# RMSNorm with swish on one core: transfers of 4 MB in place of 2 MB, same ring, same compute pieces

## The chip, the cores and the metric

The kernel runs on one core of a Trainium2 chip. The metric is the device time of one execution in microseconds (us).

Engines: ACT (ScalarE), DVE (VectorE), POOL (GpSimd), SP (SyncE, which here only issues loads), and 16 DMA engines that move data between the chip's main memory and its on-chip memory. TensorE is not used.

## The reference

```python
# x: 16 x 1024 x 512 float32, gamma: 512 ones, eps = 1e-5
rms = np.sqrt(np.mean(x ** 2, axis=-1, keepdims=True) + eps)
x_norm = x / rms * gamma
return (x_norm * (1.0 / (1.0 + np.exp(-x_norm)))).astype(np.float32)
```

33.55 MB come in and 33.55 MB go out.

## The kernel before

The 16384 rows of 512 floats are cut into tiles. A tile of `sz` gives each of the 128 partitions `sz` neighbouring rows, so one partition's share is one contiguous run of `sz` x 2 KB, and a tile is `sz` x 256 KB. Tiles live in one ring of 96 rows per partition (24 MB). A tile is computed in place and stored from the same place. Compute goes in pieces of 4 rows per partition (1 MB), whatever the tile's size.

```python
    sizes = [4, 4] + [8] * 15      # 1, 1, then fifteen times 2 MB
    ring = 96
    ahead = 32
    cn = 4
    # ... (cut: tiles = (first row, size, place in the ring); chunks = places of the pieces)

    def load(t):                   # the SP queue
        nc.sync.dma_start(out=buf(t), in_=dram(xf, t))

    def store(t):                  # the ACT queue
        nc.scalar.dma_start(out=dram(of, t), in_=buf(t))

    # sums(k): 3 rows of squares on ACT, 1 on DVE.  root(k): DVE, then POOL (power -0.5)
    # norm(k): 4 DVE instructions.                  swish(k): one ACT instruction
    # ... (cut)
        for k in range(K + 3):
            if k < K:
                sums(k)
                root(k)
            while stored < len(tiles) and ends[stored] <= k - 2:
                store(stored)
                stored += 1
            # ... (cut: gamma at k == 0)
            if 1 <= k <= K:
                norm(k - 1)
            if 2 <= k < K + 2:
                swish(k - 2)
                # ... (cut: further loads, as far ahead as the ring allows)
```

ACT works in program order, so a store issue stands behind the sums of a later piece. And the framework shares eight completion semaphores (the counters by which an engine learns that a transfer has landed) among all transfers: a transfer whose semaphore was used before waits at its issue until that earlier transfer, on whichever queue, has landed. A listing of the built program's instructions with their waits shows which.

## Time and profile before

| what | before |
|---|---|
| time | 164.03 us (163.86 to 164.15) |
| span of the profiled run | 162.1 us |
| bytes moved, mean rate | 67.15 MB, 414 GB/s |
| ACT, DVE busy | 118.8 us, 110.3 us |
| transfers | 17 loads, 17 stores, and gamma |

From the page of the kernel before: the busy tenths of the engines and the rate of the DMA engines, each in 40 slices of 4.05 us.

```profile
DVE  0376999998996800970088978859998999998000
ACT  3447999999996009800799889499999999996300
```

In the DMA row, a 9 is 90% busy or more.

```profile
DMA  4999999999999999999999999999999999999992
GB/s 162 439 437 449 392 376 423 437 429 419 433 425 441 429 425 437 433 425 437 433 425 437 433 425 433 437 425 433 435 414 445 429 421 441 429 425 441 429 425 121
DMA packets 4908, 67.15 MB, mean 414 GB/s; under 512 B 548, under 2 KB 548, under 8 KB 552
```

The DMA engines are full in every slice but the first and the last. ACT and DVE have holes of several slices. So this is a kernel at the pace of its transfers. The dip to 376 GB/s in the fifth and sixth slices will come up again, with the kernel after_2m_start.

The view of waits of the kernel before (engine, line, what it waited for: total us, times, longest us):

```profile
POOL rstd L97 <- DVE aeps L93: 98.5, 32, 11.9
DVE aeps L93 <- ACT junk_a L80: 32.8, 32, 9.9
ACT xb L111 <- DMA xb<-in_x_dram: 21.2, 4, 9.6
ACT junk_a L80 <- DMA xb<-in_x_dram: 6.9, 4, 2.9
```

Two lines of its timeline (start us, duration us, engine and line; in brackets the idle time before it):

```profile
60.66 0.34 ACTq L73 DMA_DIRECT2D out_dram<-xb  x1
61.04 1.91 ACT L111 ACTIVATE xb<-xb 128x2048 f32<-128x2048 f32 x1 [8.12 <-DMA xb<-in_x_dram]
```

The third line of waits looks as if swish (L111) needed a load. It does not: its data had been on the chip long before. The timeline shows a store issue directly ahead of it on ACT, and the trace has the ninth load landing at 60.58 us. The listing of waits says the same: that store reuses the semaphore of that load. Below, such a load, on which a store waits only because of the shared semaphore, is called foreign. ACT stands still for 21 us in this way, and, as the DMA row says, it costs nothing.

### The profile page before, as it was taken

What the parts mean: (1) busy time and instruction counts of PE and PEld (TensorE: products, weight loads), DVE (VectorE), ACT (ScalarE), POOL (GpSimd) and SP (SyncE); (2) the same over time, 40 slices, a digit from 0 to 9 for tenths busy, and PEclk for the clock granted to TensorE, in tenths of its full rate; (3) what the DMA queues carried; (4) which work ended last, traced back from release to release, by engine and by line L of the source; (5) the groups of instructions that cost most, each with busy time, mean ns of one, the idle gap of its engine ahead of it and who ended that gap; (6) DMA issues with size and microseconds to landing.
All of it is one profiled execution on the core that took longest, in us unless ns stands there. A gap on an engine that the chain in (4) does not pass through costs nothing.

```text
span 162.1 us, 629 instructions
## 1 busy us (share of the span) xinstructions
DVE 110.3 (68%) x226; ACT 118.8 (73%) x225; POOL 46.4 (29%) x38
## 2 busy tenths in 40 slices
DVE  0376999998996800970088978859998999998000
ACT  3447999999996009800799889499999999996300
POOL 1052433333441300330033423333333444430000
DMA  4999999999999999999999999999999999999992
GB/s 162 439 437 449 392 376 423 437 429 419 433 425 441 429 425 437 433 425 437 433 425 437 433 425 433 437 425 433 435 414 445 429 421 441 429 425 441 429 425 121
DMA packets 4908, 67.15 MB, mean 414 GB/s; under 512 B 548, under 2 KB 548, under 8 KB 552
## 3 DMA queue, kind: packets, MB, share of 16 engines
q1 hardware_dynamic: 2448, 33.56, 49.3%
q10 hardware_dynamic: 2456, 33.56, 48.4%
q14 instruction: 4, 0.03, 0.0%
HBM read 33.56 MB, written 33.55 MB: 414 GB/s over the span
## 4 chain that ended last, share of the span: by engine, by line
DMA 47%; ACT 36%; issue 4%; DVE 3%; another core or an unknown queue 1%; SPq 0%; ACTq 0%; DVEq 0%
DMA xb<-in_x_dram 36%; ACT junk_a L80 19%; ACT xb L111 17%; DMA out_dram<-xb 12%; DVE xb L104 3%; SPq L70 0%; ACTq L73 0%; DVEq L178 0%; DVE aeps L93 0%; ACTq L80 0%
## 5 line engine op out<-in xcount | busy, mean ns | idle before, releaser
L104 DVE SCALAR_TENSOR_TENSOR xb<-xb,rstd,gamma_sb 128x512 f32<-128x512 f32 x128 | 87.4, 745 | 0.0
L111 ACT ACTIVATE xb<-xb 128x2048 f32<-128x2048 f32 x32 | 60.7, 1897 | 23.1 <-DMA xb<-in_x_dram 21.2
L97 POOL TENSOR_TENSOR rstd<-aeps,neg_half 128x4 f32<-128x4 f32 x32 | 45.6, 1426 | 98.5 <-DVE aeps L93 98.5
L80 ACT ACTIVATE junk_a<-xb 128x512 bf16<-128x512 f32 x96 | 58.9, 615 | 6.9 <-DMA xb<-in_x_dram 6.9
L93 DVE TENSOR_SCALAR aeps<-ms 128x4 f32<-128x4 f32 x32 | 5.4, 170 | 32.8 <-ACT junk_a L80 32.8
L86 DVE CUSTOM_DVE_ANT_0 junk_v<-xb 128x512 bf16<-128x512 f32 x32 | 21.9, 683 | 6.0 <-DMA xb<-in_x_dram 6.0
L80 ACT ACTIVATION_READ_ACCUMULATOR junk_a<-xb 128x1 f32 x96 | 18.0, 187 | 0.0
L117 ACT ACT_TABLE_LOAD x1 | 1.3, 1283 | 2.4 <-issue 2.4
L86 DVE DVE_READ_ACCUMULATOR2_ANT ms<- 128x1 f32 x32 | 2.6, 81 | 0.0
L140 DVE STREAM_SHUFFLE gamma_sb<-gamma 128x512 f32<-128x512 f32 x1 | 0.7, 724 | 0.0
L114 POOL MEMSET gamma<- 128x512 f32 x1 | 0.5, 525 | 0.3 <-POOLq L164 0.3
L164 POOL MEMSET const-float32-0.0<- 128x1 f32 x1 | 0.1, 99 | 0.2 <-issue 0.2
L115 POOL MEMSET neg_half<- 128x4 f32 x1 | 0.1, 103 | 0.0
L164 POOL MEMSET const-bfloat16-1.0<- 128x1 bf16 x1 | 0.1, 102 | 0.0
L164 POOL MEMSET const-uint8-127<- 128x1 uint8 x1 | 0.1, 102 | 0.0
L164 POOL MEMSET const-float32-1.0<- 128x1 f32 x1 | 0.1, 99 | 0.0
L140 DVE LOAD_MASK_SELECT gamma_sb<-gamma x1 | 0.0, 14 | 0.0
## 6 DMA issues: line engine op xcount, KB each, us to landing
xb<-in_x_dram SPq DMA_DIRECT2D x15, 2048.0 KB, 44.0
out_dram<-xb ACTq DMA_DIRECT2D x15, 2048.0 KB, 17.5
xb<-in_x_dram SPq DMA_DIRECT2D x2, 1024.0 KB, 5.8
out_dram<-xb ACTq DMA_DIRECT2D x2, 1024.0 KB, 14.5
gamma<-in_gamma_dram ACTq DMA_DIRECT2D x1, 8.0 KB
```

The lines of the kernel that those rows point to most:

```text
L80: nc.scalar.activation(out=junk[:], in_=row, func=AF.Square, accum_out=ms[:, k, j : j + 1],)
L86: nc.vector.tensor_tensor_reduce(out=junk[:], in0=row, in1=row, scale=1.0, scalar=0.0, op0=ALU.mult, op1=ALU.add, accum_out=ms[:, k, j : j ...
L93: nc.vector.tensor_scalar(out=aeps[:, k, :], in0=ms[:, k, :], scalar1=inv_d, scalar2=eps_f, op0=ALU.mult, op1=ALU.add,)
L97: nc.gpsimd.tensor_tensor(out=rstd[:, k, :], in0=aeps[:, k, :], in1=neg_half[:], op=ALU.pow)
L104: nc.vector.scalar_tensor_tensor(out=row, in0=row, scalar=rstd[:, k, j : j + 1], in1=gamma_sb[:], op0=ALU.mult, op1=ALU.mult,)
L111: nc.scalar.activation(out=rows, in_=rows, func=AF.Silu)
L114: nc.gpsimd.memset(gamma4[:], 0.0)
L115: nc.gpsimd.memset(neg_half[:], -0.5)
L117: nc.scalar.preload_act_table_set("silu_and_others")
L140: nc.vector.stream_shuffle(gamma_sb[:], gamma4[:], [0] * 32)
L164: nc = _bacc.Bacc("TRN2", target_bir_lowering=False, num_devices=1)
```

## The change

The intent: fewer and larger transfers for most of the data, small ones at the start so that compute begins early, 2 MB at the end so that the last store is short.

```diff
-    sizes = [4, 4] + [8] * 15
+    sizes = [4, 4, 8] + [16] * 6 + [8, 8]
     ring = 96
     ahead = 32
     cn = 4
```

Each partition's contiguous run goes from 16 KB to 32 KB in the six large tiles; the transfers go from 17 to 11 each way.

## The prediction

> **What bounds the kernel now.** The DMA engines, over nearly all of the 162.1 us span. The page's DMA row reads 9 in all but the end slices; 67.15 MB move at a mean of 414 GB/s. ACT is busy 73%, DVE 68%. The trace's packet records say it more finely: packets start at 1.74 us, all 16 engines stay occupied until about 159 us, loads end at 132.8 us, then stores alone run at about 430 GB/s. A 16 KB packet takes 611 ns, an 8 KB one 309 ns, on either queue: 16 x 16384 B / 611 ns = 429 GB/s. The Trainium skill ("DMA: Bandwidth & Descriptors", section "Where 436 GB/s comes from") puts a ceiling of 435 GB/s there; the trace agrees within 2%.
>
> **What the change does.** Same bytes, same compute pieces, same ring. Seventeen loads and seventeen stores become eleven and eleven; rows of 16 KB per partition become 32 KB for 24 of 32 MB each way.
> - Packet overhead: from 309 and 611 ns, about 7 ns of a packet is fixed (an estimate). If 32 KB goes as one packet it takes about 1215 ns: six tiles x 2 directions x 8 packets per engine x 7 ns = 0.7 us less. If it is cut at 16 KB, nothing.
> - Issue time (0.33 to 0.5 us each, timeline) falls, off the critical path.
> - 21.2 us of ACT's swish "waiting on loads" (longest 9.6 us, view of waits) are store issues held by a load far ahead that shares their semaphore (order listing). With fewer transfers these waits go; ACT waits for whole 4 MB loads instead. Both are off the critical path while a queue is full.
> - Sharing: the queues alternate by packet (8 KB stores against 16 KB loads ran at 133 and 270 GB/s; the skill's section "Queues, rings and completion order", same page, states it). So 4 MB loads outrun the small first stores, and 4 MB stores slow the last two loads.
>
> **Is any of it on the critical path?** Only if both queues empty. I laid out a timetable from these durations (per piece: ACT 1.84 us sums and 1.80 us swish, DVE 2.7 us, POOL 1.44 us; the packet times; the waits of the order listing). For the kernel before it gives the last landing at 161.3 us (measured 161.1). For after: the fourth tile lands at about 25 us (ACT waits 5 us); the last load at 134 us; the last 4 MB store cannot be issued before that, because sums that need that load stand ahead of it on ACT, so at about 134.5 us, while the store before it drains until about 139 us. The margin is about 5 us, so no hole; the last store is issued at 147 to 149 us with a 2 MB store still ahead of it, as before. Last landing: 160.6 us with 32 KB packets, 161.1 us with 16 KB.
>
> **Prediction.** 163.5 us, range 162.4 to 164.8. Faster by over 2%: 0.02; within 2%: 0.93; slower by over 2%: 0.05.
>
> **What would show it.** DMA row at 9 in all but the end slices; 32 KB packets near 1215 ns; loads ending at 132 to 134 us; the last 4 MB store issued just after the last load lands; ACT and DVE busy times unchanged; last landing at 160 to 161.5 us.
>
> **What would make it wrong.** A slice under 9 at 135 to 145 us: the last 4 MB store came too late. Lower rates with 32 KB rows, from how addresses spread over the memory: 1% of rate is 1.6 us. A longer start.

## The result, and the profile after

| what | before | after |
|---|---|---|
| time, median of 4 runs | 164.03 us (163.86 to 164.15) | 163.12 us (162.92 to 163.41) |
| ratio, 95% interval | | 0.9947 (0.9929 to 0.9965) |
| span of the profiled run | 162.1 us | 161.1 us |
| ACT, DVE busy | 118.8, 110.3 us | 118.7, 110.7 us |
| last load lands | 133.2 us | 133.65 us |
| last store lands | 161.1 us | 160.2 us |

A ratio here is the mean time of one kernel's fast runs over that of the other's in the same rounds, so it is not quite the ratio of the medians quoted beside it. 0.9947 of 164 us is 0.87 us: small, and clear of noise.

The same rows of the page after:

```profile
DVE  0376946998999999999966998069999604990000
ACT  3447919999999999999939996099999408954000
```

```profile
DMA  5999989999899999999999999999999999999993
GB/s 171 437 435 521 390 352 488 413 403 480 366 407 431 484 411 447 399 456 447 399 447 456 399 439 464 417 415 421 431 435 464 419 403 472 415 415 423 439 415 146
DMA packets 3180, 67.15 MB, mean 417 GB/s; under 512 B 356, under 2 KB 356, under 8 KB 360
```

Do not read the jumps between 352 and 521 GB/s as a changing rate. A packet is counted whole in the slice in which it starts, and these packets take 1.2 us of a 4 us slice. Spread over its own duration, each packet gives 431 to 433 GB/s in the stretches with one kind of packet. The two 8s in the DMA row come from the same counting: with packets spread over their durations, the engines stay full.

The view of waits after, and the timeline around the issue of the last 4 MB store:

```profile
POOL rstd L97 <- DVE aeps L93: 94.1, 32, 9.2
ACT junk_a L80 <- DMA xb<-in_x_dram: 23.9, 7, 6.9
DVE junk_v L86 <- DMA xb<-in_x_dram: 19.6, 5, 5.8
```

```profile
133.73 0.63 ACT L80 ACTIVATE junk_a<-xb 128x512 bf16<-128x512 f32 x1 [6.90 <-DMA xb<-in_x_dram]
133.90 0.34 ACTq L73 DMA_DIRECT2D out_dram<-xb  x1
```

The waits of swish on foreign loads are gone. ACT now stands as long (24 us) for loads that it really needs. The last line is the one place where compute could have hurt: the last 4 MB store was ready long before, but it stands behind sums that need the last load, which landed at 133.65 us. It goes out at 133.90 us, while the store before it drains until about 139 us (on the slowest engine to 140.5 us).

### The profile page after: what moved, and what is told of

Same layout as the page of the kernel before. It is cut to its first block, busy times and chain, and to the rows that moved or that the text cites. A ratio compares the mean times of both kernels' runs of the same rounds, so it can differ in the third digit from the quotient of the medians.

```text
span 161.1 us, 612 instructions
## 1 busy us (share of the span) xinstructions
DVE 110.7 (69%) x226; ACT 118.7 (74%) x225; POOL 46.4 (29%) x38
## 4 chain that ended last, share of the span: by engine, by line
DMA 59%; ACT 20%; another core or an unknown queue 4%; issue 4%; DVE 3%; SPq 1%; DVEq 0%; ACTq 0%
DMA xb<-in_x_dram 41%; DMA out_dram<-xb 19%; ACT junk_a L80 12%; ACT xb L111 8%; DVE xb L104 3%; SPq L70 1%; DVEq L178 0%; DVE aeps L93 0%; ACTq L80 0%
## 5 line engine op out<-in xcount | busy, mean ns | idle before, releaser
L80 ACT ACTIVATE junk_a<-xb 128x512 bf16<-128x512 f32 x96 | 59.0, 615 | 23.9 <-DMA xb<-in_x_dram 23.9
```

The source lines that it names most:

```text
L80: nc.scalar.activation(out=junk[:], in_=row, func=AF.Square, accum_out=ms[:, k, j : j + 1],)
```

## The experiments

The theory (packets): the DMA engines are full all the time, so only what makes their work shorter counts. Every packet has a small fixed cost, and packets of 32 KB pay it half as often. The rivals: that fewer transfers give the gain; or that ACT's release from the foreign waits does. A second question is how far the tail was from a hole, where both queues are empty.

One measurement served all of them. After the last load stores go alone, and for some 15 us in packets of one size. Bytes over time there, each packet spread over its duration, give the pace of the engines, that is, the time from one packet to the next on one of the 16 (one profile each, trace records; windows within 128 to 156 us):

| packet | recorded duration | rate | pace = 16 x size / rate |
|---|---|---|---|
| 4 KB (before_4k) | 159 ns | 421.5 GB/s | 155.5 ns |
| 8 KB (before_8k) | 309 ns | 427.9 GB/s | 306.3 ns |
| 16 KB (before) | 611 ns | 431.1 GB/s | 608.1 ns |
| 32 KB (after) | 1213 ns | 433.1 GB/s | 1210.6 ns |

Twice one pace less the next gives the fixed part: 4.7, 4.5 and 5.6 ns. (0.2 GB/s more or less in the last row moves the last of these by 0.6 ns.) The recorded durations overlap by 2 to 4 ns, which is why the same subtraction on them gives 7 to 9 ns.

### Only the packet length put back (after_16k)

```diff
     def dram(ap, t):
-        return ap[first : first + P * sz].rearrange("(p n) d -> p n d", n=sz)
+        h = 2 if sz == 16 else 1
+        return ap[first : first + P * sz].rearrange("(h p m) d -> p h m d", h=h, p=P)
     # and the ring side as p (h m) d -> p h m d
```

The same eleven transfers each way and the same waits; each 4 MB tile is two 16 KB runs per partition.

> The changed kernel with each 4 MB transfer cut into two 16 KB runs per partition (the same eleven loads and stores, the same waits; only the packet length goes back). Packet theory: packets of 611 ns again, 16.1 of 16 engines busy, the gain mostly gone: ratio to the kernel before 0.998 to 1.000, about 163.9 us (only the 0.1 us of fewer completion packets stays). Rival, fewer transfers and no ACT waits on foreign loads: the gain stays, ratio 0.994 to 0.996.

Measured: 163.64 us, ratio 0.9985 (0.9973 to 0.9996); the large packets 611 ns at the median. Its page and its view of waits:

```profile
DMA packets 4716, 67.15 MB, mean 415 GB/s; under 512 B 356, under 2 KB 356, under 8 KB 360
ACT junk_a L84 <- DMA xb<-in_x_dram: 26.9, 9, 5.7
```

Most of the gain is gone, about 0.6 of 0.87 us. The 0.87 us are from other rounds, but in the same rounds as this run a kernel with 32 KB packets (after_4m_to_end, below) came to 0.9948. So packet length carries most of the gain. The rival "fewer transfers" is refuted as the main cause, and so is ACT's release: swish has no wait for a load in this run either. The remaining 0.25 us (0.07 to 0.44 by the interval) goes with what is left of the change at the same packet length: fewer transfers and other waits.

### Packets made shorter in the kernel before (before_8k, before_4k)

The same edit on the kernel before, with `h = 2` or `h = 4` where `sz == 8`.

> The kernel before with each 2 MB transfer cut into two 8 KB runs per partition (same transfers, same waits). Packet theory: packets of 309 ns, 15 tiles x 2 directions x 8 x 7 ns = 1.7 us more, ratio 1.009 to 1.012. Rival, transfers or waits set the time: ratio 1.000.

Measured: 165.12 us, ratio 1.0072 (1.0059 to 1.0085), so 1.2 us more. The direction is the theory's, the size is below what was expected. The fixed part was taken from recorded durations (7 ns). With the paces of the table, 240 more packets per engine cost 240 x 4.5 ns = 1.1 us, which is what came.

> The kernel before with each 2 MB transfer cut into four 4 KB runs per partition. From the pace of stores alone at the end of three traces (16 engines over 427.3, 430.7 and 432.9 GB/s for 8, 16 and 32 KB packets: 306.7, 608.6 and 1211 ns) a packet has a fixed 4.8 to 6.2 ns. Packet theory: 720 packets per engine more, 3.5 to 4.5 us more than the kernel before: about 167.9 us, ratio 1.021 to 1.028. Rival, the time of transfers is set by bytes and the small differences are noise: ratio 1.00 to 1.01.

Measured: 167.96 us, ratio 1.0246 (1.023 to 1.0261), so 4.0 us more. Of these the paces explain 240 x (4 x 155.5 - 608.1) ns = 3.3 us. The first stretch (394 against 411 GB/s in the table below) is slower than they say: with packets spread, from 7.5 to 16 us 404 GB/s came, where the pace of 4 KB packets would give 421.5, so about 0.4 us more. The last 0.3 us are not accounted for. The table by stretches (stretch, its length, busy of DVE, ACT and POOL, clock, share of the DMA engines, GB/s; the share can pass 1 because recorded durations overlap) of the kernel before and of this one:

```profile
2.00:16.00 14.00, 6.64 (x17) 8.17 (x20) 3.23 (x3) 1.00 0.97 411
24.00:132.00 108.00, 79.80 (x164) 85.26 (x166) 33.10 (x23) 1.00 1.01 430
```

```profile
2.00:16.00 14.00, 6.20 (x16) 7.73 (x20) 2.79 (x3) 1.00 0.97 394
24.00:132.00 108.00, 78.13 (x161) 83.77 (x162) 32.33 (x24) 1.00 1.02 421
```

and of before_8k and after:

```profile
24.00:132.00 108.00, 79.58 (x163) 85.11 (x164) 33.19 (x24) 1.00 1.01 427
```

```profile
24.00:132.00 108.00, 88.89 (x182) 94.61 (x182) 37.42 (x26) 1.00 1.01 432
```

With loads and stores mixed, the rate climbs 421, 427, 430, 432 GB/s from 4 KB to (mostly) 32 KB, with the engines full in each. With packets spread it is 420.7, 427.2, 430.2 and 431.1, and 430.3 for after_16k, whose packets are those of the kernel before. Packet length orders five kernels.

### Transfer count put back at 32 KB packets (after_halves)

```diff
-        nc.sync.dma_start(out=buf(t), in_=dram(xf, t))
+        step = P // 2 if tiles[t][1] == 16 else P
+        for p in range(0, P, step):
+            nc.sync.dma_start(out=buf(t)[p : p + step], in_=dram(xf, t)[p : p + step])
```

and likewise the store.

> The changed kernel with each 4 MB transfer issued as two of 64 partitions (transfers of 2 MB as before, seventeen each way, packets of 32 KB). Packet theory: packets of about 1213 ns, ratio to the kernel before about 0.995 (0.994 to 0.997). Rival, fewer transfers: the gain goes, ratio 0.998 to 1.001. If half the partitions give fewer engines or a lower rate, it will be much slower and says nothing for either.

Measured: 227.72 us, ratio 1.385. (Two of six runs, the profiled one among them, were slow, near 235 us; the ratio uses the fast ones.) As the expectation allowed, this says nothing about the count of transfers. Transfers of 64 partitions still used all 16 engines (272 completion packets for 17 loads), and the engines were occupied until about 180 us, but in the profile, which is of a slow run, a 32 KB load packet took 2041 ns at the median instead of 1213. Why, no run here tells. The page of its profiled run:

```profile
DMA packets 3372, 67.15 MB, mean 288 GB/s; under 512 B 548, under 2 KB 548, under 8 KB 552
```

### More work on ACT in the middle (after_act_busy)

```diff
+            if 5 <= k <= 20:
+                for _ in range(2):
+                    spare = junk_pool.tile([P, D], bf16, name="spare")
+                    nc.scalar.activation(out=spare[:], in_=gamma_sb[:], func=AF.Square)
             if k < K:
                 sums(k)
```

> The changed kernel with two spare squares of 128x512 on ACT ahead of each piece from the 6th to the 21st (32 in all, about 0.6 us each, 18 to 20 us of ACT work; results unused). DMA theory: ACT fills its 24 us of waits for loads, every store of the last four tiles is still issued before the queue empties; DMA row 9 throughout; ratio to the kernel before 0.994 to 0.997, as without it. Rival, the gain came from ACT being held less (21 us of store issues behind foreign loads): the gain goes or turns, ratio 0.999 or more.

Measured: 163.10 us, ratio 0.9948 (0.9935 to 0.996), the ratio of the change itself. ACT did 18 us more and waited less:

```profile
DVE 110.4 (68%) x226; ACT 136.7 (85%) x257; POOL 46.4 (29%) x38
```

```profile
ACT junk_a L80 <- DMA xb<-in_x_dram: 8.9, 4, 3.4
```

So 18 us of ACT time are worth nothing here. Together with after_16k, which has no foreign waits of swish and yet little of the gain, this leaves the rival "ACT was released" no part in the 0.6 us.

### The margin of the tail (after_late3, after_late10)

```diff
                 sums(k)
+                if k == 30:
+                    for _ in range(3):     # 10 in after_late10
+                        spare = junk_pool.tile([P, D], bf16, name="spare")
+                        nc.scalar.activation(out=spare[:], in_=gamma_sb[:], func=AF.Square)
                 root(k)
```

> The changed kernel with three spare squares on ACT between the sums of the 31st piece and the issue of the last 4 MB store: that store goes out about 3 us later (1.9 us of sums that it was dispatched ahead of, then two squares). Margin theory: the store before it drains until about 139.0 us and the margin is 4 to 5 us, so nothing changes: ratio 0.993 to 0.997. Rival, no margin (the tail is serial in ACT): 2 to 3 us more.

Measured: 163.17 us, ratio 0.9954 (0.994 to 0.9968). The store went out at 136.41 us, 2.5 us later than in the changed kernel, and nothing changed.

> The same with ten spare squares: the last 4 MB store goes out 7 to 8 us later, at about 141.5 us. Margin theory: a hole of 7.6 minus 4.3 us, a slice of the DMA row under 9 at about 139 to 142 us, time 163.1 + 3.3 = 166.4 us (165.6 to 167.4). Rival, serial tail: 169 us or more. Rival, no effect: 163.1 us.

Measured: 164.80 us, ratio 1.0056 (1.0037 to 1.0076): 1.7 us over the changed kernel's median. A hole there is; the cost is below the expected range (165.6 to 167.4 us). The timeline line, and the rows of the page, in which the slice with a 3 is that from 138.7 to 142.8 us:

```profile
141.41 0.34 ACTq L73 DMA_DIRECT2D out_dram<-xb  x1
```

```profile
DMA  5999989989999999999999999999999999399796
GB/s 167 442 438 498 385 353 474 458 359 470 452 393 426 410 450 434 450 401 442 458 393 474 418 426 450 400 440 430 438 422 438 442 450 410 145 385 514 321 450 257
```

Why cheaper? The mean engine was idle for 2.9 us from 136 to 144 us (occupied 13.6 and 6.8 of 16 in two stretches of 4 us). But the engines do not finish together. The completion packets of the last store, one on each engine, came at 158.35 to 159.87 us in the changed kernel and at 161.81 to 161.98 us in this one. The laggard ended 2.1 us later, the first ones 3.5 us later. The kernel ends with its last engine, and a hole in front of everyone lets the laggard catch up: part of the hole is filled from the 1.5 us by which the engines were apart. (In the trace all engines are idle from about 141 to 142 us; after that they end within 0.2 us of each other.) My expectation had taken all engines to drain at once.

### 4 MB up to the end (after_4m_to_end) and 2 MB at the start (after_2m_start)

```diff
-    sizes = [4, 4, 8] + [16] * 6 + [8, 8]
+    sizes = [4, 4, 8] + [16] * 7          # after_4m_to_end
+    sizes = [8, 8] + [16] * 7             # after_2m_start
```

> The changed kernel with the last two 2 MB tiles joined to one of 4 MB. My timetable: last load lands about 124.5 us, the store before the last is issued at about 132 and the last at about 145 us, while stores queued before them drain until about 139 and 148.6 us, so no hole, and another 0.1 us of packets saved: ratio 0.993 to 0.996. Rival, a 4 MB tile at the end leaves compute exposed: a slice under 9 after 135 us and 166 us or more.

Measured: 163.23 us, ratio 0.9948 (0.9936 to 0.996). Last load at 124.22 us, the last two stores issued at 131.72 and 144.62 us, no hole. The timetable held within a microsecond; the further 0.1 us cannot be told from nothing.

> Transfers of 2, 2 and seven of 4 MB. Two questions. One: load packets ran up to 0.6 us long for some microseconds from 18 us on in every run, just after the first store; here the first store is issued at about 24 us. If the first store brings it, the long packets move to about 25 us; if it is a matter of time or of the load's place, they stay at 18 to 22 us. Two: packets and transfers fall by another 0.1 us, but my timetable has the last 4 MB store issued at about 148.2 us, with the queue empty at about 148.8 us less about 1 us of start: a hole of 0.5 us at the mean engine, and less at the engine that ends last. Time 162.8 to 163.5 us, ratio 0.993 to 0.997.

Measured: 163.28 us, ratio 0.9958 (0.9946 to 0.9971). The last store was issued at 147.57 us and no loss can be seen. The first question has a clear answer. Load packets over their usual duration (the dip in the rates of the page before) lay mostly at 18 to 22 us in the kernel before and in the changed one (first store issued at 16.8 us), and at 25 to 29 us, with some at 32 to 33 us, here (first store issued at 23.8 us). In this one test they follow the first store. In sum they cost about 0.8 us per engine in the kernel before and 0.5 us in the changed one (excess over 611 or 1213 ns, single profiles). What in the first stores does it, no run here tells.

### 8 MB transfers (after_64k)

```diff
-    sizes = [4, 4, 8] + [16] * 6 + [8, 8]
+    sizes = [4, 4, 8, 16, 32, 32, 16, 8, 8]
```

> Loads and stores of 1, 1, 2, 4, 8, 8, 4, 2, 2 MB: 64 KB per partition in half of the data. Packet theory by itself: another 32 packets per engine fewer, 0.2 us less (162.9 us). My timetable: 64 KB stores take most of the turns from the last 16 KB loads, the last load lands only at about 140 us with the store queue already empty, and the 4 MB store held behind it on ACT leaves a hole of about 3 us: 165.7 us (164.5 to 167). If the hardware cuts packets at 32 KB or less, the last load lands earlier and the hole is smaller or none.

Measured: 166.83 us (165.80 to 167.15), ratio 1.0168 (1.014 to 1.0195). Packets of 64 KB do exist, recorded at 2418 ns, so the hardware did not cut them. The last load lands at 143.19 us, later still than the expected 140 us: a 64 KB store packet holds an engine four times as long as a 16 KB load packet (2418 against 611 ns), and from 100 to 139 us the stores moved 313 GB/s and the loads 100. The 4 MB store behind it on ACT goes out only then:

```profile
143.27 0.63 ACT L80 ACTIVATE junk_a<-xb 128x512 bf16<-128x512 f32 x1 [10.33 <-DMA xb<-in_x_dram]
143.44 0.34 ACTq L73 DMA_DIRECT2D out_dram<-xb  x1
```

```profile
140.00:148.00 8.00, 3.45 (x8) 4.73 (x10) 1.44 (x1) 1.00 0.61 260
```

The engines were 61% occupied in that stretch; with packets spread over their durations, the mean engine was idle for about 3.2 us. This kernel is 3.7 us slower than the changed one, but the hole is not all of it: in after_late10 a hole of 2.9 us cost 1.7 us. In the profile (of the slowest of the four runs) the engines moved only 413 GB/s from 104 to 136 us, fully occupied, against 431 in the changed kernel, because many packets ran beyond their usual durations; that is 1.4 us more. What slowed them, no run here tells. So the time fell into the expected range in part by luck: the hole was forecast, the slow packets were not.

No experiment gave a version clearly better than the changed kernel; two tied with it.

## Why the prediction was right

- **What bounds the kernel.** Right. The DMA engines were full before and after, and 18 us more of ACT work cost nothing.
- **The time.** 163.5 us was predicted (162.4 to 164.8), 163.12 us came; 0.5 us of gain was said, about 0.9 us measured. The range also holds the time before, 164.03 us, so lying in it says little; the terms below say more.
- **The packet term.** Right in kind: 32 KB went as one packet, recorded at 1213 ns (1215 was said). As a size, "7 ns of a packet is fixed" was from durations that overlap; the paces give 4.5 to 5.6 ns. 96 packets fewer per engine are then 0.5 us, not 0.7 us; after_16k, which undoes the packet length alone, gave 0.6 us back.
- **A term left out.** The sum had nothing for fewer transfers. after_16k shows 0.25 us (0.07 to 0.44) beside the packet length. The trace has 12 completion packets of 9 ns fewer per engine, 0.1 us. The slow-down at the first stores was milder too: from 16 to 24 us, with packets spread, 390 GB/s in the kernel before, 395 in after_16k and 406 in the changed one. Against the kernel before that is 0.1 and 0.3 us (estimates from these rates). So it may give the rest of the 0.25 us, and some 0.2 us of after_16k's 0.6 us may be this and not the fixed part of packets. These are single profiles: argued, not shown.
- **The semaphore waits.** Right: the 21.2 us of swish behind foreign loads vanished, 23.9 us of waits for needed loads took their place, and neither counts (after_16k, after_act_busy).
- **Sharing by turns.** Right. In the changed kernel 8 KB stores beside 32 KB loads moved at about 90 against 340 GB/s (21 to 44 us), near 1 to 4. The Trainium skill says so ("DMA: Bandwidth & Descriptors", section "Queues, rings and completion order": the engines go round the queues packet by packet); the trace agrees.
- **The tail.** Right: last load 133.65 us (134 said), last 4 MB store issued at 133.90 us (134.5 said), last store issued at 146.8 us (147 to 149 said), last landing 160.2 us (160.6 said). Early in the kernel the timetable was off by more: the fourth tile landed at 23.6 us (25 said), and ACT waited 3.3 us for it (5 said). The margin of about 5 us was tested: 2.5 us later is free, 7.5 us later is not. What was wrong in the expectation of after_late10 was only the price of the hole.

## What to carry to other kernels

When the DMA engines are full from end to end, count their packets: here each has about 5 ns of fixed cost beside 600 ns per 16 KB, so doubling a 16 KB run is worth about half a percent. Before enlarging transfers, lay out a timetable of the end and ask which store issue stands behind which load; an issue that leaves later than the queue runs dry costs up to its delay. The kernel with 8 MB transfers lost 3.7 us, in part to such a hole and in part to packets that ran long, where the packets saved were worth 0.2 us (an estimate from 32 packets of 5 to 6 ns). A wait that the profile shows on an idle engine may be a store issue held by a shared semaphore; see what stands ahead of it before you shorten it, and whether it matters at all.

## What the Trainium skill lacked or had wrong

- "DMA: Bandwidth & Descriptors", section "Where 436 GB/s comes from", says that for transfers between main memory and on-chip memory about 358 GB/s binds. Without a condition that is not so: this kernel, on one core and reading and writing at once, held 430 to 431 GB/s for over 100 us, near that section's 435 GB/s ceiling (what the neighbouring core did is not on record). The "HBM Reference", section "Specifications (TRN2)", has the condition: about 358 GB/s with both cores of a pair streaming, about 425 GB/s for a core that streams alone, which these runs slightly exceed.
- "DMA: Bandwidth & Descriptors", section "Why small descriptors are slow", gives a fixed cost of about 3 cycles per packet, and 32 bytes of descriptor data for each operation besides. At the 850 MHz and 32 bytes per cycle of its section "Where 436 GB/s comes from" that would be 3.5 ns and about 1.2 ns (estimates); the runs show 4.5 to 5.6 ns for packets of 4 to 32 KB and can't tell the two apart. So nothing is wrong there, but the section finds the joining of descriptors worth it only at 256 B and less. The page has no figure for the gain from 16 KB to 32 KB (0.5%).
- The same DMA page, section "Rules for kernel authors", says of two transfers to disjoint partition halves only that they gain nothing, since they share the engines. Here they were far worse: ratio 1.385 in the fast runs, and 32 KB load packets at 2041 ns instead of 1213 in the profile of a slow run.
- No page read here says that load packets slow down for some microseconds at the first stores: 0.3 to 0.8 us per engine over eleven profiles, moving from 18 us to 25 us with the first store in the one run that moved it.
- "DMA: Bandwidth & Descriptors", section "Latency and other measured facts", calls two of the 16 engines usually slower and guesses at the other way of issuing transfers (from GpSimd) as the cause. Here all transfers of x, gamma and out are issued from SP and ACT, and a few engines still end last: in the changed kernel fourteen completion packets of the last store came from 158.35 to 158.96 us, the other two at 159.31 and 159.87 us. In the nine profiles of fast runs without a hole in the tail, two engines (seven times) or three (twice) ended at least 0.3 us after the rest. The trace does not number the engines, so whether they are the same two stays open.
